# Seven half-size products for eight in the first feed-forward product, with its result kept in DRAM

## The chip, the core and the metric

The kernel runs on one core of one Trainium2 chip. The metric is the device time of one execution in microseconds, as the median of several runs.

## What is computed

One encoder block on 512 tokens of 2048 channels, all in float32: a modulated norm, a wide input projection, two mixers (state space and Fourier), a gated merge, an output projection, and then a SwiGLU feed-forward part. Only the last part matters here:

```python
h2 = modulate(rms_norm(x, norm_ffn[l]), sh_f, sc_f)          # 512 x 2048
a, b = jnp.split(h2 @ w_ffn_in[l], 2, axis=-1)                 # 2048 x (2 * 5632)
x = x + g_f[:, None, :] * ((jax.nn.silu(a) * b) @ w_ffn_out[l])  # 5632 x 2048
return rms_norm(x, norm_final)
```

## The kernel before

Every large product is made from split operands: a float32 matrix is held as `hi` (its value rounded to the format that TensorE reads at full rate, `F32R`) and `lo` (what the rounding left). `split` (line 121) makes them: ScalarE copies to `hi` (L122), VectorE subtracts to `lo` (L123). `mm3` (line 194) issues three matmuls for one product: `hi` by `hi`, `hi` by `lo`, `lo` by `hi` (L196, L197, L198).

The program is a list of steps. Each step has a job (the load of a block of weights of 512 KB, and its preparation, mostly a split) and a function that issues the matmuls. `run_plan` (line 151) writes the steps out: loads go out as early as the slots of a ring of five raw tiles allow, preparations up to three steps ahead (`LOOKAHEAD`). TensorE and GpSimd keep the order written; the orders of ScalarE and VectorE are laid down when the program is built, by priority and expected readiness. SyncE issues the weight loads in order.

The first feed-forward product has 88 output tiles of 128 channels: 44 of `a` and 44 of `b`. `first_fn` (line 1431) makes the first four tiles while the normed input `h2` (16 pairs of `hi` and `lo` tiles, 128 channels by 512 tokens) is still being formed. From line 1455 each tile is made by `ntile` (line 467) in two steps; a step has 8 of the 16 parts of the contraction, that is 24 matmuls with 128x128 weights and 512 moving columns, into one PSUM bank. Then `silu_epi` (line 1398, ScalarE, L1401) or `g_epi` (line 1405, VectorE, L1407) takes the tile out of PSUM, and `g`, the product of the two, stays in SBUF (44 x 512 floats for each partition). Between the tiles 32 steps of `gf_q` (line 1410) form the last modulation vector on VectorE (L283), with 512 KB of weights each, and four times `ada_fin` (line 323) has TensorE add it up.

`fo_open` (line 1462) has GpSimd load what the end needs. Then the second product runs twice over the 44 parts of its contraction, once for each half of the output columns: `fo_job` (line 1485) loads 512 KB of weights and splits them and a tile of `g`; the matmuls (L1509 to L1511) fill all eight PSUM banks (`fo_alloc`, line 1513).

Of the kernel before, what the change touches and what calls it, by code (L numbers as in the profile page):

```python
# [11 lines left out]
F32 = mybir.dt.float32  # L12
F32R = mybir.dt.float32r
# [6 lines left out]
P = 128  # L20
# [31 lines left out]
def encoder_block(ctx: ExitStack, tc: tile.TileContext, x, c, w_ada, b_ada, norm_mix, w_in,  # L52
# [44 lines left out]
    CAP = {"raw": RAW_BUFS, "wh": WH_BUFS, "araw": ARAW_BUFS, "bw": 2, "rv": 2, "acc": 1, "acc2": 2}  # L97

    class Job:
        """A load, and a preparation of what it brought; `raw`, `keep`: the ring slots that each takes.  # L100
        `lead`: steps that the load comes earlier in order; `late`: steps that the result is kept longer.
        The raw slots are free when the job has been prepared (those of `raw_free`), or when it has run
        (`hold`); the others when it has run."""

        def __init__(self, load, prep, raw=(("raw", 1),), keep=(("wh", 1),), raw_free=None, hold=False, free=None):
            self.lead = self.late = 0
            self.load, self.prep, self.raw = load, prep, raw
# [37 lines left out]
    def step(job, fn, barrier=False):  # L145
        """One step of the plan; no weights are prepared ahead of a barrier."""
        if barrier:
            barriers.add(len(steps))
        steps.append((job, fn))

    def run_plan():
# [3 lines left out]
        ld = pp = 0  # L155
# [3 lines left out]
        def fits(slots):  # L159
            return all(used[r] + k <= CAP[r] for r, k in slots)  # L160

# [4 lines left out]
        for i in range(n):  # L166
            moved = True
            while moved:
                moved = False
                while ld < len(order) and fits(steps[order[ld]][0].raw):  # L170
                    j = order[ld]
                    take(steps[j][0].raw, 1)
# [4 lines left out]
                while pp < n and pp <= i + LOOKAHEAD and not (pp in barriers and pp >= i) and (  # L177
                        steps[pp][0] is None or (pp in arrived and fits(steps[pp][0].acq))):
                    job = steps[pp][0]
                    if job is not None:  # L180
                        take(job.acq, 1)
                        prepped[pp] = job.prep(loaded.pop(pp))
                        take(job.at_prep, -1)
# [47 lines left out]
    def bcast_cols(r, dst):  # L231
        """[P, 4] over (token in a tile, tile) -> a row of 512 tokens on every partition."""
# [13 lines left out]
    sgr = drp.tile([KT, P], F32, name="sgr")  # L246

# [1 line left out]
    ada_acc = {}  # L249

    def ada_job(sec, c0, width, q, start=False):
        """Part q of a block of columns: some rows of each partition's 16."""
# [37 lines left out]
        return Job(load, prep, raw=(("araw" if start else "raw", 1),), keep=slot if q == 0 else (),  # L290
                   free=slot if q == parts - 1 else ())

    def ada_pe(width, then):
        """The first columns of the scale, on the tensor engine."""
# [40 lines left out]
    def ada_steps(sec, c0, width=S, start=False, then=None):  # L335
# [5 lines left out]
        return [(ada_job(sec, c0, width, q, start), last if q == parts - 1 else nop) for q in range(parts)]  # L341

# [55 lines left out]
    # The shift of the modulation comes later than its scale: the first output tiles are computed  # L398
    # without it, and what it adds to them is a vector.
# [67 lines left out]
    def ntile(wv, n0, acts, epilogue, inter=None):  # L467
        """Two steps: 128 output channels from column n0 over a contraction of 2048; `inter` is called
        after each of the 16 parts of the contraction."""
# [18 lines left out]
    def spread(tile_steps, extra):  # L488
        """The extra steps behind the two of a tile, evenly."""
# [14 lines left out]
    class Deferred:  # L504
        """Vector operations that are issued a few at a time."""
# [1125 lines left out]
```

## Time and profile before

| | |
|---|---|
| median of 3 runs | 2599.86 us (2590.38 to 2600.63) |
| span of the profiled execution | 2596.6 us |
| TensorE busy in it | 2494.6 us (96%) |
| VectorE, ScalarE, GpSimd busy | 1327.8, 763.0, 415.2 us |
| moved by DMA | 399.32 MB |

The profiled execution has no time of its own beside its span; the span lies within the runs, 3.3 us under their median. Matmuls are pipelined, so that a record of a matmul overlaps the next one's, and "busy" says only that there was no gap. What a matmul costs is read from the distance between the starts of two of them. The trace calls the engines PE (TensorE matmuls), PEld (its weight loads), DVE (VectorE), ACT (ScalarE), POOL (GpSimd) and SP (SyncE).

### The profile page before, as it was taken

Reading aid. Unit: us, or ns where it says so; the run is one execution under the profiler, and the core shown is the slowest. Engines: PE = TensorE matmul, PEld = TensorE weight load, DVE = VectorE, ACT = ScalarE, POOL = GpSimd, SP = SyncE. Lnnn points to the kernel's source line nnn. Section 1 sums busy time; section 2 is a strip of 40 time slices with the busy share of each in tenths; the row PEclk is TensorE's granted clock in tenths of the full one; section 3 lists DMA queues with packets and bytes.
Section 4 is the critical chain, followed back from the end, with each engine's and each line's share of the span. In section 5 each row is a group of like instructions: output and inputs, shape, how many; then the busy total and the mean of one; then the engine's idle time right before and its main releaser. Section 6 shows DMA issues by size and latency. Waiting matters only on the chain.

```text
span 2596.6 us, 29781 instructions
## 1 busy us (share of the span) xinstructions
PE 2494.6 (96%) x11595; PEld 2069.6 (80%) x11595; DVE 1327.8 (51%) x1718; ACT 763.0 (29%) x1097; POOL 415.2 (16%) x523
## 2 busy tenths in 40 slices
PE   6989899899999899999999999999999999999997
PEld 5767687788888787788888888888888888888886
DVE  6988467537667987773333333333322233345335
ACT  4434333243223422252222222222222222223223
POOL 2441989500005410000000000000000030001001
PEclk7989899999999999999999999999999999999999
DMA  8796522558774668863443434444433352333222
GB/s 309 260 313 142 126 78 84 177 154 266 244 219 153 186 216 282 270 204 114 122 122 117 121 113 130 122 119 120 121 97 96 97 195 97 97 98 98 98 97 81
DMA packets 460253, 399.32 MB, mean 154 GB/s; under 512 B 46384, under 2 KB 372544, under 8 KB 460112
## 3 DMA queue, kind: packets, MB, share of 16 engines
q1 hardware_dynamic: 428720, 361.60, 45.1%
q10 hardware_dynamic: 21952, 18.96, 2.7%
q0 software_dynamic: 9440, 16.86, 1.9%
q8 instruction: 91, 1.49, 0.2%
q14 instruction: 50, 0.41, 0.1%
HBM read 372.10 MB, written 29.37 MB: 155 GB/s over the span
## 4 chain that ended last, share of the span: by engine, by line
PE 67%; DVE 11%; DMA 9%; POOL 6%; issue 4%; ACT 2%; SPq 0%; ACTq 0%; DVEq 0%; POOLq 0%
PE ps_acc L196 15%; PE ps_acc L198 15%; PE ps_acc L197 15%; DMA raw<-in_w_in_dram 3%; PE ps_acc L1510 3%; PE ps_acc L1511 3%; PE ps_acc L1509 3%; DVE wlo L123 3%; DMA raw<-in_w_out_dram 3%; DVE ada L283 2%; PE ps_accb L1509 1%; PE ps_m L1509 1%; PE ps_m L1511 1%; PE ps_m L1510 1%; PE ps_accb L1511 1%
## 5 line engine op out<-in xcount | busy, mean ns | idle before, releaser
L123 DVE TENSOR_TENSOR wlo<-raw,whi 128x1024 fp32r<-128x1024 f32 (+2 forms) x424 | 521.6, 1232 | 593.4 <-ACT whi L122 592.9
L122 ACT CAST whi<-raw 128x1024 fp32r<-128x1024 f32 (+2 forms) x424 | 428.4, 1011 | 1043.3 <-PE ps_acc L197 767.4
L198 PE MATMUL ps_acc<-actB,wlo 128*128 128x512 f32 x1776 | 698.0, 393 | 7.6 <-DVE wlo L123 7.6
L196 PE MATMUL ps_acc<-actB,whi 128*128 128x512 f32 x1776 | 703.2, 396 | 1.0 <-ACT actB L122 0.5
L197 PE MATMUL ps_acc<-actB,whi 128*128 128x512 f32 x1776 | 697.4, 393 | 0.9 <-DVE actB L123 0.9
L198 PEld LDWEIGHTS ps_acc<-actB,wlo 128*128 128x128 f32 x1776 | 337.0, 190 | 82.0 <-DVE wlo L123 10.6
L196 PEld LDWEIGHTS ps_acc<-actB,whi 128*128 128x128 f32 x1776 | 337.7, 190 | 72.8 <-issue 2.5
L197 PEld LDWEIGHTS ps_acc<-actB,whi 128*128 128x128 f32 x1776 | 337.1, 190 | 69.6 <-DVE actB L123 1.6
L196 PE MATMUL ps_acc<-actA,whi 128*128 128x512 f32 x592 | 237.9, 402 | 2.1 <-ACT actA L122 2.1
L198 PE MATMUL ps_acc<-actA,wlo 128*128 128x512 f32 x592 | 235.4, 398 | 2.2 <-DVE wlo L123 2.1
L283 DVE SCALAR_TENSOR_TENSOR ada<-raw,c_s,ada 128x512 f32<-128x512 f32 x240 | 181.2, 755 | 108.6 <-DMA raw<-in_w_ada_dram 104.1
L197 PE MATMUL ps_acc<-actA,whi 128*128 128x512 f32 x592 | 235.5, 398 | 0.9 <-DVE actA L123 0.9
L123 DVE TENSOR_TENSOR actA<-g,actA 128x512 fp32r<-128x512 f32 x88 | 61.9, 708 | 260.6 <-ACT actA L122 260.6
L1467 POOL DMA_DIRECT2D sgr<-gr x1 | 0.5, 541 | 1186.4 <-ACT gr L1466 1186.4
L122 ACT CAST actA<-g 128x512 fp32r<-128x512 f32 x88 | 54.5, 623 | 310.8 <-PE ps_m L1510 310.8
L1510 PE MATMUL ps_acc<-wlo,actA 128*128 128x512 f32 x352 | 137.2, 390 | 0.8 <-DVE wlo L123 0.8
L1509 PE MATMUL ps_acc<-whi,actA 128*128 128x512 f32 x352 | 137.1, 389 | 0.0
L1511 PE MATMUL ps_acc<-whi,actA 128*128 128x512 f32 x352 | 137.0, 389 | 0.0
L198 PEld LDWEIGHTS ps_acc<-actA,wlo 128*128 128x128 f32 x592 | 113.9, 192 | 27.8 <-DVE wlo L123 3.4
L196 PEld LDWEIGHTS ps_acc<-actA,whi 128*128 128x128 f32 x592 | 113.4, 192 | 25.6 <-ACT actA L122 2.2
L197 PEld LDWEIGHTS ps_acc<-actA,whi 128*128 128x128 f32 x592 | 113.6, 192 | 24.0 <-DVE actA L123 1.4
L1407 DVE TENSOR_TENSOR g<-silu,ps_acc 128x512 f32<-128x512 f32 x44 | 30.3, 688 | 124.9 <-PE ps_acc L198 124.9
(391 smaller groups left out, 3165.8 us busy)
## 6 DMA issues: line engine op xcount, KB each, us to landing
raw<-in_w_ffn_in_dram SPq DMA_DIRECT2D x168, 512.0 KB
raw<-in_w_ada_dram SPq DMA_DIRECT2D x128, 512.0 KB
raw<-in_w_in_dram SPq DMA_DIRECT2D x108, 512.0 KB
raw<-in_w_ffn_out_dram SPq DMA_DIRECT2D x88, 512.0 KB
araw<-in_w_ada_dram SPq DMA_DIRECT2D x64, 512.0 KB
raw<-in_w_out_dram SPq DMA_DIRECT2D x32, 512.0 KB
raw<-in_w_in_dram SPq DMA_DIRECT2D x16, 384.0 KB
rv<-wrev SPq DMA_DIRECT2D x16, 384.0 KB
```

Source lines behind the costliest of these rows:

```text
L122: A.copy(hi, src)
L123: V.tensor_tensor(out=lo, in0=src, in1=hi.bitcast(F32), op=ALU.subtract)
L196: PE.matmul(o, whi, ahi, start=start, stop=False)
L197: PE.matmul(o, whi, alo, start=False, stop=False)
L198: PE.matmul(o, wlo, ahi, start=False, stop=stop)
L283: V.scalar_tensor_tensor(out=acc, in0=r[:, k, :], scalar=sc, in1=acc, op0=ALU.mult, op1=ALU.add)
L1407: V.tensor_tensor(out=ff["g"][:, j, :], in0=ff.pop(("s", j)), in1=pt, op=ALU.mult)
L1467: nc.gpsimd.dma_start(out=sgr, in_=gr)
L1509: PE.matmul(o, gh[:, ts_], hi[:, cs], start=(k == 0), stop=False)
L1510: PE.matmul(o, gh[:, ts_], lo[:, cs], start=False, stop=False)
L1511: PE.matmul(o, gl[:, ts_], hi[:, cs], start=False, stop=(k == NF - 1))
```

## The change

Of the 88 output tiles of the first feed-forward product, 8 (of `a` and `b`, j under 4) are made as before, and the other 80 in 40 pairs of neighbours. For one pair the 256 output channels, the 512 tokens and the 2048 channels of the contraction are each cut in two, and the eight products of halves are replaced by seven products of sums and differences of halves. `form_sums` makes the four combinations of `h2` once, beside the direct tiles j = 2 and 3. `quad_job` loads 512 KB of weights (a quarter of the contraction for 256 channels), takes three of their four blocks as they are (`hi` by a ScalarE copy; `lo` as a negated ScalarE copy of the rounded value, to which a DMA issued by GpSimd adds the raw value), and makes four combinations of the blocks on VectorE, which are split as before. Each quarter is 42 matmuls of 256 moving columns. After four quarters the pair is put together from PSUM by one ScalarE and five VectorE instructions into two SBUF tiles.

`g` is written to DRAM (`sg`) by DMAs that ScalarE issues, and `fo_job` loads it again, one tile of 256 KB with each block of weights, in both passes. The planner gets slots for this, and a rule that a raw slot stays free for the sums. The diff, without removed comments and less some bookkeeping:

```diff
+           "quad": 3, "ada": 1, "sum": 2, "gr": 2}
...
-                while ld < len(order) and fits(steps[order[ld]][0].raw):
+                while ld < len(order):
                     j = order[ld]
+                    job = steps[j][0]
+                    if not fits((*job.raw, ("raw", 1)) if job.raw and (open_ or job.opens) else job.raw):
+                        break
+                    open_ += job.opens
...
+                        open_ -= job.closes
...
+    sg = drp.tile([NF, P, S], F32, name="sg")
...
     step(None, norm2)
+    DIRECT = 4
+    H = S // 2
+    def ab_tile():
+        return ff["p"].tile([P, S], F32, tag="ab", bufs=4, name="ab")
     def silu_epi(j):
         def fn(pt):
-            s = cpool.tile([P, S], F32, tag="tmp", bufs=3, name="silu")
+            s = ff["s", j] = ab_tile()
             A.activation(out=s, in_=pt, func=AF.Silu)
-            ff["s", j] = s
         return fn
     def g_epi(j):
         def fn(pt):
-            V.tensor_tensor(out=ff["g"][:, j, :], in0=ff.pop(("s", j)), in1=pt, op=ALU.mult)
+            s = ff.pop(("s", j))
+            V.tensor_tensor(out=s, in0=s, in1=pt, op=ALU.mult)
+            A.dma_start(out=sg[j], in_=s)
         return fn
-    gf_q = [st_ for cb in range(4) for st_ in ada_steps(5, cb * S)]
+    def form_sums(p):
+        f = ff["p"].tile([P, 2, 2, H], F32, tag="hT", bufs=2, name="h2f")
+        for i in range(2):
+            hi, lo = h2[2 * p + i]
+            V.tensor_tensor(out=f[:, i].rearrange("p a b -> p (a b)"), in0=hi.bitcast(F32), in1=lo.bitcast(F32),
+                            op=ALU.add)
+        a12, a22, a11, a21 = f[:, 0, 0], f[:, 0, 1], f[:, 1, 0], f[:, 1, 1]
+        t = ff["p"].tile([P, 4, H], F32, tag="lT", bufs=2, name="sumf")
+        V.tensor_tensor(out=t[:, 0], in0=a21, in1=a22, op=ALU.subtract)
+        V.tensor_tensor(out=t[:, 2], in0=a11, in1=a21, op=ALU.subtract)
+        V.tensor_tensor(out=t[:, 1], in0=a11, in1=t[:, 0], op=ALU.subtract)
+        V.tensor_tensor(out=t[:, 3], in0=t[:, 1], in1=a12, op=ALU.subtract)
+        hl = [ff["p"].tile([P, 4, H], F32R, name=f"sum{p}{i}") for i in range(2)]
+        split(hl[0], hl[1], t)
+        ff["S", p] = hl
+    def quad_job(c, n0):
+        st = {}
+        def load():
+            st["r"] = raw_tile([P, 2, 4, P])
+            nc.sync.dma_start(out=st["r"].rearrange("p a (b n) c -> p (a b) (n c)", b=2),
+                              in_=w_fi_v[:, 4 * c:4 * c + 4, n0:n0 + 2 * P])
+            return st["r"]
+        def prep(r):
+            hi, lo = hl_tiles([P, 2, 3, P])
+            A.copy(hi, r[:, :, 0:3])
+            A.activation(out=lo, in_=r[:, :, 0:3], func=AF.Copy, scale=-1.0)
+            G.dma_start(out=lo, in_=r[:, :, 0:3], accum_op=ALU.add)
+            st["w"] = (hi, lo)
+        job = Job(load, prep, raw=(("raw", 1), ("quad", 1)), raw_free=())
+        job.late, job.opens = 1, True
+        def prep_sums(_):
+            r = st["r"]
+            t = raw_tile([P, 2, 4, P])
+            V.tensor_tensor(out=t[:, :, 0:2], in0=r[:, :, 1:3], in1=r[:, :, 3:4].to_broadcast([P, 2, 2, P]), op=ALU.add)
+            V.tensor_tensor(out=t[:, :, 2], in0=t[:, :, 1], in1=r[:, :, 1], op=ALU.add)
+            V.tensor_tensor(out=t[:, :, 3], in0=t[:, :, 2], in1=r[:, :, 0], op=ALU.add)
+            hi = ff["p"].tile([P, 2, 4, P], F32R, tag="hT", bufs=2, name="hT")
+            lo = ff["p"].tile([P, 2, 4, P], F32R, tag="lT", bufs=2, name="lT")
+            split(hi, lo, t)
+            return (*st["w"], hi, lo)
+        sums = Job(lambda: None, prep_sums, raw=(), keep=(("sum", 1), ("raw", 1)), raw_free=(("raw", 2), ("quad", 1)),
+                   free=(("sum", 1),))
+        sums.closes = True
+        return job, sums
+    def quad_tiles(n0, epilogue):
+        st = {}
+        def fn_of(c):
+            def fn(w):
+                hr, lr, ht, lt = w
+                if c == 0:
+                    st["37"], st["24"], st["16"], st["5"] = (
+                        f((P, 2, H)) for f in (ps_acc, ps_acc, ps_b, ps_m))
+                plan = [("16", 0, True, (hr, lr), 2, None, (1, 0)), ("24", 0, True, (hr, lr), 0, None, (0, 0)),
+                        ("37", 0, True, (hr, lr), 1, 3, None), ("5", 0, True, (ht, lt), 1, 0, None),
+                        ("37", 1, False, (ht, lt), 0, 2, None), ("16", 1, False, (ht, lt), 2, 1, None),
+                        ("24", 1, False, (ht, lt), 3, None, (0, 1))]
+                for bank, half, opens, (wh, wl), q, s_, raw in plan:
+                    o = st[bank][:, half]
+                    for i in range(2):
+                        p = 2 * c + i
+                        if raw is None:
+                            ah, al = (x[:, s_] for x in ff["S", p])
+                        else:
+                            ah, al = (x[:, raw[1] * H:(raw[1] + 1) * H] for x in h2[2 * p + raw[0]])
+                        first, last = c == 0 and i == 0, c == 3 and i == 1
+                        PE.matmul(o, wh[:, i, q], ah, start=first and opens, stop=False, skip_group_check=True)
+                        PE.matmul(o, wh[:, i, q], al, start=False, stop=False, skip_group_check=True)
+                        PE.matmul(o, wl[:, i, q], ah, start=False, stop=last, skip_group_check=True)
+                if c < 3:
+                    return
+                ez = cpool.tile([P, 2, H], F32, tag="tmp", bufs=3, name="ez")
+                uw = cpool.tile([P, 2, H], F32, tag="tmp", bufs=3, name="uw")
+                A.copy(ez[:, 0], st["16"][:, 0])
+                V.tensor_tensor(out=uw[:, 0], in0=st["16"][:, 1], in1=ez[:, 0], op=ALU.subtract)
+                V.tensor_tensor(out=uw[:, 1], in0=st["5"][:, 0], in1=uw[:, 0], op=ALU.add)
+                V.tensor_tensor(out=ez[:, 1], in0=st["37"][:, 1], in1=uw[:, 0], op=ALU.subtract)
+                b2 = ab_tile()
+                V.tensor_tensor(out=b2.rearrange("p (a b) -> p a b", a=2), in0=uw[:, 1:2].to_broadcast([P, 2, H]),
+                                in1=st["37"], op=ALU.subtract)
+                a2 = ab_tile()
+                V.tensor_tensor(out=a2.rearrange("p (a b) -> p a b", a=2), in0=st["24"], in1=ez, op=ALU.add)
+                epilogue(a2, b2)
+            return fn
+        out_ = []
+        for c in range(4):
+            job, sums = quad_job(c, n0)
+            out_ += [(job, nop), (sums, fn_of(c))]
+        return out_
+    def silu2(j):
+        def fn(*tiles):
+            for i, t in enumerate(tiles):
+                A.activation(out=t, in_=t, func=AF.Silu)
+                ff["s", j + i] = t
+        return fn
+    def g2(j):
+        def fn(*tiles):
+            for i, t in enumerate(tiles):
+                g_epi(j + i)(t)
+        return fn
+    gf_q = [st_ for cb in range(4) for st_ in ada_steps(5, cb * S, extra=(("ada", 1),))]
     pairs = [(ntile(w_fi_v, j * P, lambda: h2, silu_epi(j)), ntile(w_fi_v, DFF + j * P, lambda: h2, g_epi(j)))
-             for j in range(NF)]
+             for j in range(DIRECT)]
     first = []
     def first_job(kk):
...
                     mm3(first[n], (hi[:, k % 2, n % 2, cs], lo[:, k % 2, n % 2, cs]), h2[k], k == 0, k == KT - 1)
             if kk == KT // 2 - 1:
                 x1x.close()
-                ff["g"] = ffx.enter_context(tc.tile_pool(name="ffp", bufs=1)).tile([P, NF, S], F32, name="g")
+                ff["p"] = ffx.enter_context(tc.tile_pool(name="ffp", bufs=1))
                 for j in range(2):
                     silu_epi(j)(first[2 * j])
                     g_epi(j)(first[2 * j + 1])
     for kk in range(KT // 2):
         step(first_job(kk), first_fn(kk))
-    for j in range(2, NF):
-        steps.extend(spread(pairs[j][0], some(gf_q, 1) if j >= 4 else []) + pairs[j][1])
+    for j in range(2, DIRECT):
+        for i, (job, fn) in enumerate(pairs[j][0] + pairs[j][1]):
+            p = 4 * (j - 2) + i
+            step(job, lambda w, fn=fn, p=p: (fn(w), form_sums(p)))
+    for j in range(DIRECT, NF, 2):
+        for n0, epi in ((j * P, silu2(j)), (DFF + j * P, g2(j))):
+            tl = quad_tiles(n0, epi)
+            steps.extend(tl[:4] + some(gf_q, 1) + tl[4:])
     assert not gf_q
     fo = {"x2": {}, "gf": [], "nf": []}
     def fo_open(_):
         def load():
             r = raw_tile([P, 1024])
             nc.sync.dma_start(out=r, in_=src)
-            return r
-        def prep(r):
+            gr = ab_tile()
+            nc.sync.dma_start(out=gr, in_=sg[k])
+            return r, gr
+        def prep(rg):
+            r, gr = rg
             hi, lo = hl_tiles([P, 1024])
             split(hi, lo, r)
             gh, gl = act_tile(0), act_tile(0)
-            split(gh, gl, ff["g"][:, k, :])
+            split(gh, gl, gr)
             return hi, lo, gh, gl
-        job = Job(load, prep)
+        job = Job(load, prep, raw=(("raw", 1), ("gr", 1)))
         job.late = NF - 1 - k if k >= NF - LAST[half] else 0
         return job
```

## Rows read from the trace of the kernel before

**Rows 1.** The page's first lines: the span, and TensorE's busy time.
```profile
span 2596.6 us, 29781 instructions
...
PE 2494.6 (96%) x11595; PEld 2069.6 (80%) x11595; DVE 1327.8 (51%) x1718; ACT 763.0 (29%) x1097; POOL 415.2 (16%) x523
```
**Rows 2.** Stretches: start, first product (two), second product; columns as in the header.
```profile
core 0: us, PE busy (x) PEld busy (x) DVE busy (x) ACT busy (x) POOL busy (x), PEclk, DMA share, GB/s
0.00:200.00 200.00, 163.95 (x707) 135.08 (x708) 167.58 (x318) 84.30 (x134) 75.66 (x57) 0.87 0.86 293
1180.00:2094.00 914.00, 914.00 (x4050) 757.50 (x4049) 280.59 (x282) 199.86 (x216) 0.00 (x0) 1.00 0.39 115
1250.00:1450.00 200.00, 200.00 (x889) 165.75 (x888) 64.05 (x65) 42.27 (x45) 0.00 (x0) 1.00 0.41 120
2140.00:2330.00 190.00, 190.00 (x840) 157.38 (x839) 67.15 (x70) 54.65 (x70) 0.00 (x0) 1.00 0.30 97
```
**Rows 3.** Waits from 1200 to 2100 us; engine, line, waited for: total us, times, longest.
```profile
ACT whi L122 <- PE ps_acc L197: 705.0, 165, 5.3
DVE wlo L123 <- ACT whi L122: 388.0, 132, 5.1
...
SPq L135 <- DVE wlo L123: 477.4, 127, 5.9
```
**Rows 4.** Timeline of TensorE, first product: two starts, 24 matmuls apart.
```profile
1580.08 0.39 PE L197 MATMUL ps_acc<-actB,whi 128*128 128x512 f32 x1
...
1585.52 0.39 PE L197 MATMUL ps_acc<-actB,whi 128*128 128x512 f32 x1
```
**Rows 5.** Timeline of TensorE, branch product: two starts, 17 matmuls of 258 columns apart.
```profile
910.74 0.28 PE L196 MATMUL ps_accb<-ab,whi 128*128 128x258 f32 x1
...
912.78 0.28 PE L198 MATMUL ps_accb<-ab,wlo 128*128 128x258 f32 x1
```
**Rows 6.** Groups from 1180 to 2094 us, shapes apart: count, busy us, mean ns, idle before.
```profile
L123 DVE TENSOR_TENSOR wlo<-raw,whi 128x1024 fp32r<-128x1024 f32 x168 | 205.7, 1224 | 398.9 <-ACT whi L122 398.7
L196 PEld LDWEIGHTS ps_acc<-actB,whi 128*128 128x128 f32 x1003 | 188.3, 188 | 38.8
L122 ACT CAST whi<-raw 128x1024 fp32r<-128x1024 f32 x167 | 175.3, 1050 | 712.0 <-PE ps_acc L197 712.0
L283 DVE SCALAR_TENSOR_TENSOR ada<-raw,c_s,ada 128x512 f32<-128x512 f32 x60 | 45.1, 752 | 97.1 <-DMA raw<-in_w_ada_dram 96.0
L1407 DVE TENSOR_TENSOR g<-silu,ps_acc 128x512 f32<-128x512 f32 x43 | 29.6, 687 | 121.6 <-PE ps_acc L198 121.6
L1401 ACT ACTIVATE silu<-ps_acc 128x512 f32<-128x512 f32 x44 | 26.0, 591 | 2.0 <-PE ps_acc L198 2.0
```
**Rows 7.** Groups of the whole span, shapes apart: other sizes on VectorE and ScalarE.
```profile
L123 DVE TENSOR_TENSOR actA<-g,actA 128x512 fp32r<-128x512 f32 x88 | 61.9, 708 | 260.6 <-ACT actA L122 260.6
L123 DVE TENSOR_TENSOR wlo<-wp,whi 128x768 fp32r<-128x768 f32 x16 | 24.7, 1541 | 2.5 <-ACT whi L122 2.4
L123 DVE TENSOR_TENSOR blo<-rv,bhi 128x768 fp32r<-128x768 f32 x16 | 15.0, 940 | 0.0
L123 DVE TENSOR_TENSOR ab<-ps_accb,ab 128x258 fp32r<-128x258 f32 x12 | 5.0, 423 | 13.4 <-ACT ab L122 13.4
...
L122 ACT CAST bhi<-rv 128x768 fp32r<-128x768 f32 x16 | 13.3, 832 | 6.2 <-POOL rv L1247 6.2
L122 ACT CAST v<-ps_m 128x258 fp32r<-128x258 f32 x24 | 9.0, 373 | 33.0 <-PE ps_m L198 33.0
```
**Rows 8.** Groups of GpSimd: DMAs that it issues, by program line.
```profile
L1476 POOL DMA_DIRECT2D actB<-sx x16 | 8.7, 547 | 6.6 <-DMA actB<-in_norm_final_dram 3.4 <-issue 1.7 <-DMA actB<-sx 1.0
L998 POOL DMA_DIRECT2D wrev<-in_w_branch_fnet_dram x6 | 6.8, 1138 | 0.0
```
**Rows 9.** DMA issues: what, queue, count, KB each, median us to landing.
```profile
wrev<-in_w_branch_fnet_dram POOLq DMA_DIRECT2D x6, 1016.0 KB, 19.8
...
sxT<-xT POOLq DMA_DIRECT2D x4, 1024.0 KB, 6.1
```
**Rows 10.** Timeline where the products meet: VectorE beside DMAs that GpSimd issues.
```profile
2101.37 0.69 DVE L1407 TENSOR_TENSOR g<-silu,ps_acc 128x512 f32<-128x512 f32 x1 [3.36 <-PE ps_acc L198]
...
2108.34 1.23 DVE L123 TENSOR_TENSOR wlo<-raw,whi 128x1024 fp32r<-128x1024 f32 x1 [0.26 <-ACT whi L122]
...
2108.45 1.62 POOL L1471 DMA_DIRECT2D actB<-in_norm_final_dram  x3
```

More of the change, by code (lines that the diff above doesn't have):

```diff
@@ L95, in encoder_block @@
     barriers = set()
-    CAP = {"raw": RAW_BUFS, "wh": WH_BUFS, "araw": ARAW_BUFS, "bw": 2, "rv": 2, "acc": 1, "acc2": 2}
+    CAP = {"raw": RAW_BUFS, "wh": WH_BUFS, "araw": ARAW_BUFS, "bw": 2, "rv": 2, "acc": 1, "acc2": 2,
+           "quad": 3, "ada": 1, "sum": 2, "gr": 2}
     class Job:
@@ L106, in __init__ @@
             self.lead = self.late = 0
+            self.opens = self.closes = False
             self.load, self.prep, self.raw = load, prep, raw
@@ L154, in run_plan @@
         used = dict.fromkeys(CAP, 0)
-        ld = pp = 0
+        ld = pp = open_ = 0
         order = sorted((i for i in range(n) if steps[i][0] is not None), key=lambda i: (i - steps[i][0].lead, i))
@@ L159, in fits @@
         def fits(slots):
-            return all(used[r] + k <= CAP[r] for r, k in slots)
+            need = {}
+            for r, k in slots:
+                need[r] = need.get(r, 0) + k
+            return all(used[r] + k <= CAP[r] for r, k in need.items())
         def take(slots, sign):
@@ L246, in encoder_block, with ada_job @@
     sgr = drp.tile([KT, P], F32, name="sgr")
+    sg = drp.tile([NF, P, S], F32, name="sg")
     ada_acc = {}
-    def ada_job(sec, c0, width, q, start=False):
+    def ada_job(sec, c0, width, q, start=False, extra=()):
         rows_ = 1024 // width
@@ L289, in ada_job @@
         slot = (("acc2" if start else "acc", 1),)
-        return Job(load, prep, raw=(("araw" if start else "raw", 1),), keep=slot if q == 0 else (),
+        return Job(load, prep, raw=(("araw" if start else "raw", 1), *extra), keep=slot if q == 0 else (),
                    free=slot if q == parts - 1 else ())
@@ L333, in nop, with ada_steps @@
         pass
-    def ada_steps(sec, c0, width=S, start=False, then=None):
+    def ada_steps(sec, c0, width=S, start=False, then=None, extra=()):
         def last(_):
@@ L340, in ada_steps @@
         parts = KT * width // 1024
-        return [(ada_job(sec, c0, width, q, start), last if q == parts - 1 else nop) for q in range(parts)]
+        return [(ada_job(sec, c0, width, q, start, extra), last if q == parts - 1 else nop) for q in range(parts)]
     s5x = ExitStack()
```

## The prediction, as it was put on record

> **What bounds the kernel now.** I read the page's engine line first, then the stretches, then who waits for whom, and last the timeline of TensorE. TensorE is busy for 96% of the span [rows 1], and in the first feed-forward product, from 1180 to 2094 us, for all of it, at a granted clock of 1.00, which is the level of 2.4 GHz; VectorE has 281 of these 914 us, ScalarE 200, GpSimd nothing, and the DMA engines are taken 0.39 of the time [rows 2]. The waits say the same: ScalarE waits 705 us for TensorE to give a weight buffer back, VectorE for ScalarE, and SyncE for VectorE to free a raw tile [rows 3]. Everything is early and TensorE sets the end. So a microsecond of TensorE taken out here is a microsecond of the kernel, as long as the others stay early.
>
> **What TensorE saves.** Two starts that lie 24 matmuls apart differ by 5.44 us: a matmul of 512 columns costs 0.2267 us [rows 4]. Two tiles of 128 channels take 2 x 16 x 3 = 96 of them, 21.76 us; 40 such pairs 870.5 us. After the change a pair takes 4 quarters x 7 products x 2 x 3 = 168 matmuls of 256 columns. The nearest row has 258 columns, the same 128x128 weights and the same three matmuls for a product: 17 of them in 2.04 us, 0.1200 us each [rows 5]. The 254 columns between the two rows cost 0.1067 us, so two columns less is 0.1192 us, and 12 ns of each matmul do not shrink with it. A pair then takes 20.03 us, 40 pairs 801 us, and the saving is 69.5 us, or 1.73 us a pair. Seven for eight alone would give 870.5 / 8 = 109 us; 40 us of it go into the fixed 12 ns. I take the measured spacing.
>
> There are 72 more weight loads in a pair. Their record lasts 188 ns [rows 6], but a matmul of 258 columns with a new load each time still starts every 120 ns [rows 5], so loads are hidden at this width. The Trainium skill (TensorE: Matmul & The Clock Gate, "The mechanism" in Part 3) says that a weight load overlaps running matmuls only where its row group differs; by this, loads of all 128 rows would not be hidden, and the change would lose. The spacing in this trace speaks against it; as a rival it stands below.
>
> **What VectorE gets.** In each quarter (5.01 us of TensorE): sums of weights of 512, 256 and 256 elements, 0.71 + 2 x 0.42 us, and the subtraction for the split of 1024, 1.22 us [rows 6, 7]; 2.77 us. For each pair: three PSUM instructions of 256 at 0.42 and two of 512 at 0.69, 2.64 us; half of two products for g at 0.71, 0.71 us; and in 32 of 40 pairs two steps of the modulation at 0.75, 1.50 us [rows 6, 7]. Together 4 x 2.77 + 4.85 = 15.9 of 20.03 us, 80%. That is twice as full as before and still not the bound. A row of 768 elements that took 0.94 us took 1.54 us where GpSimd computed beside it [rows 7]; times 1.64 VectorE would need 26 us a pair and be the bound. But GpSimd only issues DMAs here, and beside those a subtraction of 1024 took 1.23 us [rows 10], the same as 1.22. I take 80%.
>
> Does it come in time? The buffers of the split sums come in two, so those of quarter c+1 can be written when quarter c-1 has ended, and are first read by the fourth of the seven products of c+1, 5.01 + 18 x 0.119 = 7.2 us later. The worst quarter is the first of a pair: the five PSUM instructions (ScalarE 0.37, then 2.64 us), the two products for g (1.4), and then the subtraction (1.22) end after some 5.9 us with the hops between engines. That is 1.3 us early. The next quarter has 12 us for two subtractions and the sums. So I put the cost of VectorE at nothing; if its work were a quarter longer this cover would be gone, and the 1 to 2 us a pair that are late would eat the 1.73 us.
>
> **ScalarE and its queue.** Two copies of 768 (0.83 each) and one of 1024 (1.05) in a quarter, one of 256 (0.37) and one silu (0.59) a pair [rows 6, 7]: 11.8 of 20.03 us. The stores of g wait in its queue for VectorE's product; the copies for the next quarters stand behind them, with over 5 us to spare. Two stores in 40 us: nothing.
>
> **The accumulating DMA** is the one price that the trace does not have. Per quarter GpSimd issues one DMA that adds 384 KB of raw values into `lo`. Issuing costs 0.55 to 1.14 us [rows 8] of an idle engine. The move itself: from below, 1024 KB from SBUF land in 6.1 us, 2.3 us for 384 KB; from above, 1016 KB from DRAM to DRAM land in 19.8 us, 7.5 us for 384 KB [rows 9]. A gain is excluded, since the bytes were not moved before. An addition has to read both sides, so I take twice the lower value, 4.6 us, the SBUF row being the nearer one. It has to fit into 5.01 us, and it does; about two quarters of lead hide its latency.
>
> Seen as a share of the DMA engines: 120 GB/s took 0.41 with 512-byte rows and 97 GB/s took 0.30 with 4 KB rows [rows 2], so all of them move 293 to 323 GB/s; I take 308. Weights need 105 GB/s, the modulation 26, the stores of g 13: 144, or 0.47. The accumulation's 78.5 GB/s are 0.255 as a copy and 0.51 as two: 0.98 in all. This is at the edge. The start of the kernel ran at 0.86 and 293 GB/s [rows 2]. I put 5 us for queueing (bounds 0 and 25).
>
> The Trainium skill (Collectives: The Full Stack, "The bandwidth ceiling") says that an adding transfer is slower than a copy since it needs two source reads, and reports the ratio as 1.93. No run here shows it yet; by it the share would be 0.96.
>
> **The rest.** Eight `form_sums` put 4.3 us of VectorE beside each 5.44 us step that has 1.22 already: 0.1 us too much in each step, needed only later; 2 us (0 to 4). At the end of the last pair two of four first-tag banks are held until its five VectorE instructions are done, 3 us, against 1.4 us of matmuls that have banks; 2 us. Before, that tile's product of 0.69 us [rows 10] held one bank. The second product loads 256 KB more for each 512 KB on SyncE's queue: 145 GB/s or 0.47 of the engines in place of 0.30, with two loads ahead, over 10 us; nothing. `fo_open`'s DMAs on GpSimd queue behind the last accumulations, done by then.
>
> Sum on the profiled execution: 2596.6 - 69.5 + 5 + 2 + 2 = 2536. The runs' median is 3.3 us over its span, so 2539 for a measured time.
>
> **The rivals.**
> A. The accumulation costs more than two copies, the DMA engines become the bound, and TensorE waits for `lo`. It decides where 0.47 + 0.255 k, times 801 us, exceeds 870.5 us: k = 2.42 copies, or 5.44 us for one DMA. At k = 3 the share is 1.235, the stage 989 us, and the kernel 2600 + 119 + 4 = 2723; at the upper row's 7.5 us it is 1200 us, some 2930. For it: the estimate at k = 2 has no margin. Against: the low row already holds fixed time and other traffic. Chance 0.22; this is the slower one.
> B. The cover on VectorE is thin: chains between ScalarE and VectorE or a DMA share a little above 1 eat 0.6 to 1.7 us a pair. Time 2563 to 2607, around 2585. For it: 80% and a static order, and the DMA share of 0.98. Against: 1.3 us of slack in the worst quarter. Chance 0.20, half within 0.5%.
> C. The change does not do what it says: 256 columns do not come at 0.119 us, because weight loads show. 72 x 0.188 = 13.5 us a pair, 541 us in all, some 3070. The row of 258 columns speaks against it. Chance 0.02.
> My forecast, 2520 to 2560: 0.56.
>
> **How the numbers follow.** 0.5% is 13 us, about what a measurement of this kernel tells from no change. Faster by more: 0.56 + 0.10 = 0.66; within: 0.10; slower: 0.22 + 0.02 = 0.24. The predicted time is the forecast's, 2539. The low end 2518 is the saving with the 12 ns a little smaller and no new cost. The high end leaves out the dear half of A: 2.6 copies give a stage of 908 us, 2641; I take 2650.
>
> **What would show it.** Right: 256-column matmuls 0.119 us apart, a pair every 20 us, the granted clock at 1.00, VectorE at 80% and the DMA share near 0.95 in the stage, the second product as long as before. For A: gaps before the matmul that reads `lo`, released by the DMA on GpSimd's queue, a landing time over 10 us, a share of 1. For B: gaps before the fourth product, released by the subtraction on VectorE. For C: no gaps, but a wider spacing. The forecast is wrong if a quarter takes over 5.4 us.

## The result and the profile after

| | before | changed |
|---|---|---|
| median | 2595.47 us (2590.38 to 2600.63, 4 runs) | 2563.39 us (2557.31 to 2566.06, 4 runs) |
| ratio, with its 95% interval | | 0.9863 (0.9837 to 0.9889) |
| span of the profiled execution | 2596.6 us | 2561.7 us |
| first feed-forward product in it | 962.5 us | 928.2 us |

The kernel is faster by 32 us, where 61 were forecast. The time lies 3 us past the forecast's own range (2520 to 2560), at the cheap end of rival B (2563 to 2607). Of the 34.9 us between the two spans 34.3 lie in the first product; the work behind it takes 496.1 us in place of 495.2.

First the page of the changed kernel: span, engines, and the one group that is new in kind, with its DMA issue.

```profile
span 2561.7 us, 37880 instructions
...
PE 2437.8 (95%) x14475; PEld 2157.9 (84%) x14475; DVE 1674.1 (65%) x2454; ACT 1030.5 (40%) x1465; POOL 605.9 (24%) x683
...
L1463 POOL DMA_DIRECT2D wlo<-raw x160 | 192.4, 1203 | 948.6 <-ACT wlo L1462 566.6
...
wlo<-raw POOLq DMA_DIRECT2D x160, 384.0 KB, 5.7
```

Next the timeline of TensorE in the changed kernel, two starts that lie 35 matmuls of 256 columns apart.

```profile
1457.73 0.28 PE L1509 MATMUL ps_acc<-sum,hT 128*128 128x256 f32 x1
...
1461.93 0.28 PE L1511 MATMUL ps_acc<-sum,wlo 128*128 128x256 f32 x1
```

4.20 us for 35 of them: 0.1200 us each, as the 258 columns of [rows 5], and a pair of 168 takes 20.16 us. Read pair by pair from the starts, 20 of the 40 take 20.15 or 20.16 us. The others take 20.5 to 25.9.

The stretches say which pairs those are. In the view below (start, end and length; then the busy time of each engine with its count of records, the granted clock, the DMA share and GB/s) the row from 1900 us holds the last eight pairs. They have the same quarters and the same accumulating DMAs as all others, and no modulation step. The row below it is from the second product.

```profile
core 0: us, PE busy (x) PEld busy (x) DVE busy (x) ACT busy (x) POOL busy (x), PEclk, DMA share, GB/s
1230.00:1390.00 160.00, 154.99 (x1252) 154.17 (x1251) 107.23 (x173) 82.41 (x103) 35.83 (x30) 0.97 0.87 205
1390.00:1550.00 160.00, 156.34 (x1282) 155.28 (x1281) 116.26 (x188) 85.05 (x108) 36.06 (x30) 0.99 0.88 211
1550.00:1710.00 160.00, 156.17 (x1293) 155.03 (x1291) 110.33 (x179) 80.95 (x103) 36.06 (x30) 1.00 0.89 213
...
1900.00:2060.00 160.00, 160.00 (x1336) 160.00 (x1335) 110.47 (x175) 91.44 (x114) 36.07 (x30) 1.00 0.87 199
...
2100.00:2300.00 200.00, 200.00 (x884) 165.68 (x883) 73.05 (x79) 57.69 (x76) 1.48 (x1) 1.00 0.46 150
```

TensorE stands still for 3.7 to 5.0 us in each 160 us of modulated pairs, and not at all in the last eight. VectorE is as full in both, and so are the DMA engines (0.87 to 0.89). The second product has the 0.46 that was forecast as 0.47, and no gap.

The 839.9 us of the 40 pairs therefore divide into 806.4 at 0.1200 us, 24.7 in 28 gaps of more than 0.15 us, and 8.8 in matmuls that start further apart than 0.12 us without a gap, 6.4 of them at the lower clock that is shown below. Of the gaps 3.2 us belong to the ends of modulation blocks, which the kernel before has too. The other 21.5 stand in or just ahead of the fourth product of a pair's last quarter.

Who waits for whom, changed kernel, 1180 to 2060 us (engine, line, waited for: total us, times, longest):

```profile
POOL wlo L1463 <- ACT wlo L1462: 566.6, 133, 10.2
ACT hT L124 <- DVE raw L1474: 174.0, 56, 8.8
DVE ada L295 <- DMA raw<-in_w_ada_dram: 125.0, 28, 7.2
DVE lT L125 <- ACT hT L124: 78.9, 47, 5.3
...
PE ps_m L1511 <- DVE lT L125: 9.7, 14, 0.8
...
PE ps_m L1509 <- ACT hT L124: 7.6, 6, 2.3
```

and SyncE's own queue, 1230 to 2060 us:

```profile
SPq L1455 <- DMA wlo<-raw: 391.1, 91, 9.0
SPq L1455 <- DMA raw<-in_w_ada_dram: 178.7, 28, 8.5
SPq L1455 <- DVE raw L1474: 112.9, 44, 3.2
```

Before, SyncE waited for VectorE's subtraction to free a raw tile [rows 3]. Now what it waits for most is the accumulating DMA, which is the last to read the tile. VectorE waits 4.5 us at 28 of the 32 modulation steps for their 512 KB. Before, it waited 96.0 us for the same loads [rows 6], and there it cost nothing, since VectorE was busy for 281 of 914 us [rows 2].

One such gap, from the timeline of the changed kernel (start, length, engine, line, operation; in brackets the idle time before it and what ended it):

```profile
1444.11 0.61 SPq L273 DMA_DIRECT2D raw<-in_w_ada_dram  x1
...
1446.13 0.69 DVE L1472 TENSOR_TENSOR raw<-raw 128x512 f32<-128x512 f32 x1
1452.60 0.75 DVE L295 SCALAR_TENSOR_TENSOR ada<-raw,c_s,ada 128x512 f32<-128x512 f32 x1 [5.78 <-DMA raw<-in_w_ada_dram]
1453.27 0.42 DVE L1473 TENSOR_TENSOR raw<-raw 128x256 f32<-128x256 f32 x1
1453.61 0.75 DVE L295 SCALAR_TENSOR_TENSOR ada<-raw,c_s,ada 128x512 f32<-128x512 f32 x1
1454.27 0.42 DVE L1474 TENSOR_TENSOR raw<-raw 128x256 f32<-128x256 f32 x1
...
1454.80 1.05 ACT L124 CAST hT<-raw 128x1024 fp32r<-128x1024 f32 x1 [7.32 <-DVE raw L1474]
...
1455.88 1.22 DVE L125 TENSOR_TENSOR lT<-raw,hT 128x1024 fp32r<-128x1024 f32 x1
...
1456.12 0.28 PE L1510 MATMUL ps_m<-sum,hT 128*128 128x256 f32 x1
1457.16 0.39 PE L1511 MATMUL ps_m<-sum,lT 128*128 128x256 f32 x1 [0.76 <-DVE lT L125]
```

The sums of this quarter are three VectorE instructions, L1472 to L1474. The modulation step stands between the first and the second of them in VectorE's order, and its weights come 5.78 us late. So the third sum ends at 1454.7, the rounding on ScalarE at 1455.9, the subtraction at 1457.1, and TensorE, which needs its result, stops.

After the larger gaps the clock adds to the loss. Two stretches of the changed kernel, columns as above:

```profile
1348.00:1351.00 3.00, 0.50 (x2) 0.30 (x2) 2.90 (x6) 2.02 (x3) 0.00 (x0) 0.93 0.50 172
1351.00:1359.00 8.00, 7.67 (x42) 7.67 (x43) 7.76 (x16) 4.49 (x7) 2.40 (x2) 0.60 0.86 171
```

TensorE idled for 2.5 of 3 us, and then ran at a mean granted clock of 0.60, mostly at 0.5, which is the level of 1.2 GHz, before it was back at 1.00. In those 8 us it did 42 matmuls, which take 5.0 us at 0.12. This happened four times, for 3.4 to 6.8 us each.

### The profile page after: what moved, and what is told of

Read it like the earlier page. It is cut to its first block, busy times and chain, and to the rows that moved or that the text cites. A ratio compares the mean times of both kernels' runs of the same rounds, so it can differ in the third digit from the quotient of the medians.

```text
span 2561.7 us, 37880 instructions
## 1 busy us (share of the span) xinstructions
PE 2437.8 (95%) x14475; PEld 2157.9 (84%) x14475; DVE 1674.1 (65%) x2454; ACT 1030.5 (40%) x1465; POOL 605.9 (24%) x683
## 4 chain that ended last, share of the span: by engine, by line
PE 50%; DVE 18%; DMA 14%; issue 7%; POOL 6%; ACT 4%; SPq 0%; ACTq 0%; DVEq 0%; POOLq 0%
DMA raw<-in_w_ada_dram 6%; PE ps_acc L207 4%; PE ps_acc L208 4%; PE ps_acc L209 4%; DMA raw<-in_w_out_dram 3%; PE ps_acc L1656 3%; PE ps_acc L1655 3%; PE ps_acc L1657 3%; DVE ada L295 3%; DVE wlo L125 3%; PE ps_acc L1509 3%; PE ps_acc L1510 3%; PE ps_acc L1511 3%; DMA raw<-in_w_in_dram 2%; DVE lT L125 2%
## 5 line engine op out<-in xcount | busy, mean ns | idle before, releaser
L125 DVE TENSOR_TENSOR wlo<-raw,whi 128x1024 fp32r<-128x1024 f32 (+2 forms) x264 | 324.8, 1232 | 191.1 <-ACT whi L124 190.3
L1463 POOL DMA_DIRECT2D wlo<-raw x160 | 192.4, 1203 | 948.6 <-ACT wlo L1462 566.6
L124 ACT CAST whi<-raw 128x1024 fp32r<-128x1024 f32 (+2 forms) x264 | 260.5, 988 | 326.9 <-DMA raw<-in_w_out_dram 104.6
L209 PE MATMUL ps_acc<-actB,wlo 128*128 128x512 f32 x816 | 324.9, 398 | 8.1 <-DVE wlo L125 8.1
L207 PE MATMUL ps_acc<-actB,whi 128*128 128x512 f32 x816 | 329.9, 404 | 1.9 <-ACT whi L124 1.5
L208 PE MATMUL ps_acc<-actB,whi 128*128 128x512 f32 x816 | 324.1, 397 | 0.3 <-DVE actB L125 0.3
L124 ACT CAST hT<-raw 128x1024 fp32r<-128x1024 f32 x160 | 167.6, 1047 | 258.4 <-DVE raw L1474 174.0
L125 DVE TENSOR_TENSOR lT<-raw,hT 128x1024 fp32r<-128x1024 f32 x160 | 195.5, 1222 | 79.2 <-ACT hT L124 78.9
L209 PEld LDWEIGHTS ps_acc<-actB,wlo 128*128 128x128 f32 x816 | 156.9, 192 | 45.3 <-DVE wlo L125 11.3
L207 PEld LDWEIGHTS ps_acc<-actB,whi 128*128 128x128 f32 x816 | 157.8, 193 | 37.0 <-ACT whi L124 2.7
L208 PEld LDWEIGHTS ps_acc<-actB,whi 128*128 128x128 f32 x816 | 157.1, 193 | 31.4 <-DVE actB L125 0.6
L1472 DVE TENSOR_TENSOR raw<-raw 128x512 f32<-128x512 f32 x160 | 110.6, 691 | 18.9 <-DMA wlo<-raw 14.0
L207 PE MATMUL ps_acc<-actA,whi 128*128 128x512 f32 x272 | 112.9, 415 | 2.1 <-ACT actA L124 2.1
```

Source lines behind the costliest of these rows:

```text
L124: A.copy(hi, src)
L125: V.tensor_tensor(out=lo, in0=src, in1=hi.bitcast(F32), op=ALU.subtract)
L207: PE.matmul(o, whi, ahi, start=start, stop=False)
L208: PE.matmul(o, whi, alo, start=False, stop=False)
L209: PE.matmul(o, wlo, ahi, start=False, stop=stop)
L1463: G.dma_start(out=lo, in_=r[:, :, 0:3], accum_op=ALU.add)
```

## The experiments

The first expectation below names three theories, W, D and V. Two more came later and are not the rivals of the prediction. Theory S: the accumulating DMA holds the raw tile until it lands, so the ring of five tiles comes free late, SyncE's loads go out late, and the modulation step, fixed in VectorE's order, makes the sums behind it late. Theory B: the DMA engines or VectorE are too full, and any more work or bytes at this place makes gaps. All ratios are to the kernel before, with 95% intervals, and "the stage" is the 40 pairs, from the first matmul of 256 columns to the last.

### The modulation steps left out

```diff
+    V.memset(mod[5], 0.0)
...
-            steps.extend(tl[:4] + some(gf_q, 1) + tl[4:])
-    assert not gf_q
+            steps.extend(tl)
```

> Leaves out the 32 steps that form the last modulation vector in this stage (their loads, 64 VectorE instructions, 4 small groups on TensorE); the vector is zero. Theory W (VectorE stands in its fixed order before a modulation instruction whose 512 KB have not landed, 125 us in all, and the sums of the pair's last quarter come late): the stage of seven products falls from 840 us to about 807, no gaps before the fourth product of the last quarter, the clock stays at 1.00; kernel 2526 to 2534. Rival D (the DMA engines, at 0.88, are too slow for the accumulation): the share falls only by 0.08, most gaps stay; 2548 to 2560. Rival V (VectorE has too much work): as W, since 1.5 us of work a pair goes too.

2528.3 us, 0.9721 (0.9702 to 0.9741). The stage takes 806.4 us, every pair 20.16. The stretch from 1230 us on, and below it SyncE's wait in it:

```profile
1230.00:1890.00 660.00, 660.00 (x5502) 660.00 (x5502) 457.46 (x725) 373.51 (x460) 157.42 (x131) 1.00 0.87 196
```

```profile
SPq L1456 <- DMA wlo<-raw: 560.1, 115, 9.1
```

The accumulation alone, at a DMA share of 0.87 and with SyncE waiting for it even longer, costs TensorE nothing. It takes a modulation step beside it to make a gap. That rules out D as it was put, a DMA too slow for its work; W and V had forecast this time alike.

### The accumulating DMA left out

```diff
-            G.dma_start(out=lo, in_=r[:, :, 0:3], accum_op=ALU.add)
```

> Leaves out the accumulating DMA, so that lo is only the negated rounded value; all else stays. Rival D: all gaps go, 2524 to 2532. Theory W: the DMA share falls to about 0.45, so modulation loads land in 4 us rather than 8 and raw tiles come free earlier; part of the gaps goes, 2530 to 2550, and VectorE still waits some 50 us for those loads. Rival V: little change, 2555 to 2565.

2534.69 us, 0.9744 (0.9727 to 0.9761). The stage takes 809.9 us and has no gap but the 3.2 us at the ends of modulation blocks. Waits of this kernel, 1230 to 2060 us, then its stretch from 1230 us:

```profile
DVE ada L295 <- DMA raw<-in_w_ada_dram: 1.6, 3, 0.9
```

```profile
1230.00:1890.00 660.00, 660.00 (x5505) 660.00 (x5504) 487.63 (x782) 370.51 (x455) 0.00 (x0) 1.00 0.44 142
```

VectorE's wait for the modulation falls from 125.0 to 1.6 us. The time rules out V and misses D by 3 us; it lies in W's range, though W had left some 50 us of that wait. This run takes away hold and traffic together, and so does not tell S from B.

### The same DMA from another source

The DMA adds a tile that stays in place, of the same size, in place of the raw tile. The traffic remains and the raw tile is no longer held.

```diff
-            G.dma_start(out=lo, in_=r[:, :, 0:3], accum_op=ALU.add)
+            G.dma_start(out=lo..., in_=ff["S", 0][0]...[:, 0:768], accum_op=ALU.add)
```

> The accumulating DMA stays, with the same 384 KB and the same wait for lo, but it adds a fixed tile of sums instead of the raw weights, so that it no longer holds a raw tile (lo is wrong by that). Theory S (the DMA is the last reader of a raw tile, so the ring of five comes free late and the loads behind it, the modulation's above all, go out late): the gaps go, 2530 to 2542, and SyncE's waits for that DMA vanish. Theory B (its traffic, at a share of 0.88, makes every load land late): as the changed kernel, 2557 to 2568, VectorE waits over 80 us for modulation loads.

2532.44 us, 0.9739 (0.9718 to 0.9761); the stage 809.9 us, no gaps but those 3.2 us. Stretch, then VectorE's and SyncE's waits in it:

```profile
1230.00:1890.00 660.00, 660.00 (x5505) 660.00 (x5504) 486.83 (x781) 367.87 (x455) 114.28 (x131) 1.00 0.89 220
```

```profile
DVE ada L295 <- DMA raw<-in_w_ada_dram: 65.6, 28, 6.1
```

```profile
SPq L1455 <- DVE raw L1474: 295.8, 116, 6.8
```

The DMA engines are as full as in the changed kernel (0.89), the DMA lands after 6.0 us in place of 5.7, and yet the loss is gone. SyncE no longer waits for the DMA but for VectorE. VectorE still waits for the modulation, half as long, and that much does no harm. (Each of these DMAs moves the same bytes in 143 packets in place of 270; together they take 45% of the engines' time, as before.) So this traffic without the hold costs nothing here, as S has it and B has not. The traffic has a part all the same. Read from the starts, as medians over 31 pairs: the modulation's load goes out 8.9 us before TensorE begins the last quarter in the changed kernel, 10.1 us here and 11.3 us without the DMA; VectorE begins with it 6.3, 5.8 and 3.6 us later. The traffic uses up half of the time in hand, and the hold takes the rest. That a hold would do it without traffic is not shown.

### The subtraction back on VectorE

```diff
-            A.copy(hi, r[:, :, 0:3])
-            A.activation(out=lo, in_=r[:, :, 0:3], func=AF.Copy, scale=-1.0)
-            G.dma_start(out=lo, in_=r[:, :, 0:3], accum_op=ALU.add)
+            split(hi, lo, r[:, :, 0:3])
```

> lo of the three plain blocks is made by a VectorE subtraction of 768 elements, as elsewhere in the kernel, in place of a ScalarE copy and the accumulating DMA. VectorE gets 0.94 us more in each quarter: 15.9 + 3.8 = 19.7 of 20.0 us a pair. Theory W and rival V: VectorE is the bound, a pair takes 21 to 23 us, kernel 2590 to 2670. Rival D: the DMA share falls to 0.45 and the gaps go, 2525 to 2540.

2537.15 us, 0.9753 (0.973 to 0.9776); the stage 809.9 us, no gaps but those 3.2 us. Its stretch:

```profile
1230.00:1890.00 660.00, 660.00 (x5505) 660.00 (x5504) 592.87 (x911) 273.67 (x325) 0.00 (x0) 1.00 0.44 142
```

My expectation for W and V missed; the time is the one of D, which the modulation run had ruled out. VectorE is busy for 90% and TensorE never waits. So how full VectorE is does not decide alone. One thing more differs: since VectorE's orders are laid down by priority, the modulation step stands elsewhere. Counted from the end of the pair before, three sum instructions come ahead of it in 18 of 31 pairs; in the changed kernel it is one or none in 27. What that gives is not separated from the missing DMA. In a further measurement this kernel and the changed one ran on one chip.

> The changed kernel again, beside the next one on the same chip: 2557 to 2567.

> The version with the VectorE subtraction again, as the version that beats both: 2530 to 2540, 0.9 to 1.2% under the changed kernel.

The changed kernel: 2559.64 us, 0.9831 (0.9806 to 0.9856). With the subtraction on VectorE: 2536.54 us, 0.9752 (0.9733 to 0.9772). The intervals lie apart. So the negated copy and the accumulating DMA were not needed: without them the kernel takes 0.9% less than the changed one beside it, and 2.5% less than the one before.

### Traffic without a hold, on a fuller VectorE

The same edit, and each quarter two plain DMAs of 384 KB from `hi` to DRAM.

```diff
+    scr = drp.tile([8, P, 768], F32, name="scr")
...
+            split(hi, lo, r[:, :, 0:3])
+            for i_ in range(2):
+                G.dma_start(out=scr[2 * (scn[0] % 4) + i_], in_=hi...)
...
```

> The version with the VectorE subtraction (2537), plus two plain DMAs a quarter that copy the 384 KB of hi to DRAM and that nothing waits for: about the engine time of one accumulation, but no raw tile held. Theory B: the loss comes back, 2555 to 2570, with VectorE waiting over 60 us for modulation loads. Theory S: 2533 to 2545 at a DMA share of 0.8 to 0.9.

2549.31 us, 0.9809 (0.9791 to 0.9828); the stage 824.2 us with 15.2 us of gaps. Stretch and wait:

```profile
1230.00:1890.00 660.00, 650.70 (x5386) 646.82 (x5386) 576.83 (x893) 259.48 (x319) 137.11 (x256) 1.00 0.85 292
```

```profile
DVE ada L297 <- DMA raw<-in_w_ada_dram: 64.6, 28, 4.6
```

Between the ranges of the two theories. Nothing holds a raw tile here, but at 292 GB/s VectorE waits for the modulation for as long as in the kernel with the other source (65 us in all), and on a VectorE that is nearly full (576.83 of 660 us) this costs 12 us against the same kernel without the copies, whose order on VectorE is the same. So traffic alone can do it too. That VectorE had no room to catch up is the likely reason, since the other source had the same wait and no loss; but the modulation step also stands elsewhere in its order there.

### A hold without an accumulation

The subtraction on VectorE, and per quarter two chained DMAs of 128 KB from the raw tile into a spare tile, after a copy of one element on ScalarE into that tile.

```diff
...
+            sp = ff["p"].tile([P, 2, P], F32, tag="spare", bufs=1, name="spare")
+            A.copy(sp[:, 0, 0:1], hi[:, 0, 0, 0:1].bitcast(F32))
+            for i_ in range(2):
+                G.dma_start(out=sp, in_=r[:, i_, 0:2])
```

> The version with the VectorE subtraction, plus two small DMAs a quarter, one behind the other, that copy 128 KB each out of the raw tile and start after hi: a third less traffic than the accumulation's reads and writes, but the raw tile is held until they have landed, as by the accumulation. Theory S (held raw tiles make the loss): SyncE waits over 150 us for these DMAs, VectorE over 60 us for modulation loads, gaps before the fourth product come back, 2542 to 2562, at a DMA share under 0.75. Theory B (traffic): 2533 to 2541, as without them.

2755.99 us, 1.059 (1.0564 to 1.0617); the stage 1036 us, past both ranges. ScalarE's and VectorE's waits, then the stretch, 1230 to 1890 us:

```profile
ACT spare L1463 <- DMA spare<-raw: 286.9, 100, 6.2
...
DVE raw L1474 <- DMA spare<-raw: 108.2, 60, 4.3
```

```profile
1230.00:1890.00 660.00, 577.70 (x4304) 564.81 (x4303) 460.28 (x710) 225.50 (x356) 111.70 (x203) 0.91 0.47 151
```

A large loss at a DMA share of 0.47, so bytes are not what makes it. VectorE's first sum waits 108 us for a raw tile that these DMAs still read, so a hold can stop VectorE as well as SyncE. But ScalarE itself waits 287 us for the spare tile, ahead of its copies for the weights, and most of the gaps (136.7 of 159.8 us) moved to the fourth product of the second quarter. The run does not measure the hold alone and does not decide between the theories.

### The modulation's loads earlier

```diff
+    for job, _ in gf_q:
+        job.lead = 4
```

> The same work as the changed kernel; only the loads of the 32 modulation steps stand four steps (two quarters) earlier in SyncE's queue. Theory W: VectorE's wait for these loads falls from 125 us to under 30, the gaps before the fourth product go, and the kernel takes 2530 to 2540. Rival V (too much work on VectorE): no change, 2557 to 2566, since the work is the same. Rival D: no change, or slower by up to 10 us, since a raw tile is held longer.

2574.17 us, 0.9891 (0.9869 to 0.9913): not faster. VectorE's wait from 1230 to 1890 us is hardly shorter, and the gaps stand in the third quarter of the pair, no longer in the fourth:

```profile
DVE ada L295 <- DMA raw<-in_w_ada_dram: 112.7, 28, 5.9
```

```profile
1230.00:1890.00 660.00, 633.97 (x5160) 627.31 (x5158) 451.11 (x732) 340.88 (x426) 146.59 (x122) 0.99 0.87 206
```

Theory W missed; rival D's forecast, up to 10 us slower, comes nearest. The step's VectorE instructions moved forward with its load: in 27 of 31 pairs one subtraction stands between the end of the pair before and the modulation step, where the changed kernel has two. The load goes out 14.3 us before the last quarter in place of 8.9, and VectorE begins with it 8.4 us before in place of 2.3 (medians). So the load is no earlier for the instruction that waits for it; no run holds the load early and the instructions late.

### Only the way through DRAM, and fewer columns

All 88 tiles direct as before, and only `g` through DRAM:

```diff
-    DIRECT = 4
+    DIRECT = NF
...
```

> All 88 tiles direct as before; only g goes through DRAM. By the prediction the DRAM route costs nothing: 2594 to 2606, within 0.3% of the kernel before. Rival: two loads ahead instead of five, and 50% more bytes in the second product, leave TensorE waiting there: over 2610.

2596.2 us, 0.999 (0.9977 to 1.0002, 10 runs). The way through DRAM costs nothing, as the prediction had it.

Last, the kernel with the subtraction on VectorE, with 192 moving columns for 256 in the second and third quarter of each pair:

```diff
...
+                    nw = 192 if c in (1, 2) else H
...
```

> The version with the VectorE subtraction; in quarters 1 and 2 of each pair the matmuls have 192 moving columns in place of 256 (a quarter of the tokens left out there). If the spacing is columns plus a fixed part, as between 258 and 512 columns, 192 columns start every 0.092 to 0.094 us and VectorE becomes the bound (gaps). If a weight load takes 0.120 us whatever the columns, the spacing of 0.120 stays and nothing changes, 2533 to 2540.

2499.37 us in one run. Timeline of TensorE in the second quarter:

```profile
1400.42 0.25 PE L1508 MATMUL ps_accb<-actB,whi 128*128 128x192 f32 x1
...
1403.98 0.27 PE L1510 MATMUL ps_accb<-sum,lT 128*128 128x192 f32 x1
```

and its busy times in that stretch, columns as above:

```profile
1400.40:1405.00 4.60, 4.60 (x44) 4.60 (x42) 3.22 (x5) 1.88 (x2) 0.00 (x0) 1.00 0.35 118
```

The distance is 0.111 us (32 matmuls in 3.56 us), where the line through 258 and 512 columns would give 0.092. Neither expectation was met: the distance is neither 0.092 nor 0.120, and no gap came. A quarter fewer columns saves 7%.

## Why the prediction was right, and where it failed

**What bounds the kernel.** Right. Wherever the inputs were in time (four kernels), TensorE ran without a gap, and what it saved came out whole.

**What TensorE saves.** The right row, a wrong correction. The step took 0.1192 us for 256 columns, from 0.1200 for 258 and a slope; it is 0.1200. That is 0.13 us a pair, 5.4 us in all. From 512 to 256 columns the distance falls by 0.1067 us, 0.417 ns for each column, which leaves 13 ns that do not shrink, close to the 12 of the prediction. At 192 columns (0.111 us) the same slope leaves 31 ns. So the fixed part held for this change and does not hold below it.

The rival about weight loads (C) fell, and with it the sentence of the Trainium skill that was weighed there (TensorE: Matmul & The Clock Gate, "The mechanism" in Part 3): 128x128 loads and 256-column matmuls run side by side at 0.1200 us, with the load unit busy for 660.00 of 660 us.

**VectorE.** The cost of nothing for its amount of work was right: 74% in the kernel with the accumulation left out (487.63 of 660 us), 80% forecast. The sentence that a quarter more work would end the cover found no support: with 22% more (592.87 us for 487.63), at 90%, there was no gap. The 1.54 us that were taken for a subtraction beside a computing GpSimd is a mean: in the trace of before, seven of these 16 ran beside GpSimd's instructions and took 1.8 to 2.6 us, the other nine 0.94 to 0.95; in this stage GpSimd does not compute, so nothing hangs on it. What the step left out of its sum is what the static order, named under rival B, does with a late input. A wait of one instruction for a DMA delays all behind it, and the 96.0 us of waits for the modulation were in the rows of before already [rows 6], where idle time covered them. The slack of 1.3 us was reckoned for the first quarter of a pair; the gaps came in the last, where the modulation step stands.

**The accumulating DMA.** Its price was nearly right, its effect was missed. In the changed kernel from 1300 to 2000 us (queue: packets, MB, share of 16 engines; then issues):

```profile
q0 software_dynamic: 36241, 52.38, 45.8%
q1 hardware_dynamic: 77515, 83.84, 37.6%
...
wlo<-raw POOLq DMA_DIRECT2D x134, 384.0 KB, 5.7
```

134 of them took 0.458 x 700 us, 2.39 us each of all 16 engines, or 164 GB/s. The loads moved 83.84 MB in 0.376 x 700 us, 318 GB/s. So one addition costs k = 1.94 copies, against the 2 that were taken and the 2.42 from which rival A decides, and close to the 1.93 of the Trainium skill (Collectives: The Full Stack, "The bandwidth ceiling"). The agreement hangs on what is called a copy. Against the 308 GB/s of the prediction k is 1.87; against the plain DMAs from `hi` to DRAM in the run with two of them (1300 to 1880 us, below), 87.91 MB in 0.406 x 580 us or 373 GB/s, it is 2.27. All lie under 2.42. The share is 0.88, not 0.98.

```profile
q0 software_dynamic: 17891, 87.91, 40.6%
```

Landing took 5.7 us, inside the bounds of 2.3 and 7.5.

The step that failed is the next one: "about two quarters of lead hide its latency". This is true for who reads `lo`. It is not true for the raw tile, which stays taken until the DMA lands, while SyncE's loads wait for it in order. Holding a tile is a cost beside moving bytes, and the sum had no term for it. The term for queueing, 5 us with bounds 0 and 25, was the only place for it, and it was too small. With the 2 and 2 for `form_sums` and the last pair the sum had 9 us; what was paid in the stage alone is 839.9 - 806.4 - 3.2 = 30.3 us, and without the hold 0.3 us (809.9 - 806.4 - 3.2). The two small terms came to 1.2 us (the direct tiles took 88.3 us for four times 21.76) and 0.9 (the work behind).

**The rivals.** B happened in its sign: gaps before the fourth product, released by VectorE's subtraction or ScalarE's copy for it, at 30.3 / 40 = 0.76 us a pair, of 0.6 to 1.7 (0.95 for each of the 32 modulated ones). Of its two causes the share above 1 did not come. A chain between VectorE and ScalarE did, but a late load set it off, which B does not name. A's rate did not happen. Without the hold the kernel lands at 2532 to 2537 us in three ways (without the DMA, with its other source, with the subtraction on VectorE), beside the 2539 that was forecast; part of that is luck, two errors that cancel, 5.4 us too little for the spacing and 7 too much for queueing and the two small terms.

**Chances.** Faster by more than 0.5% had 0.66, and the time lies inside the range of 2518 to 2650, which is wide enough to hold B; the forecast's own range, with 0.56, it misses by 3 us. The sign that was to tell a wrong forecast, a quarter over 5.4 us, shows in the last quarters that have a gap, not in the mean of 839.9 / 160 = 5.25 us.

**Open.** No run has the hold without the traffic, so how much of the 30 us it costs alone is not known. What sets the spacing at 192 columns was not found, and that row is from one run.

## What to carry to other kernels

When a copy or a subtraction is given to a DMA, ask what it still reads and until when: its landing time is added to the life of the source tile, and the next loads queue behind that. A wait for a transfer that costs nothing on an engine with time to spare can cost time once that engine feeds the bound in a fixed order: 65.6 us of such waits still cost nothing here, 125.0 us cost 30, and on a fuller VectorE 64.6 us cost 12. Look for such waits in the profile of before, and ask where they stand in the order as well as how full the engine is. Take the spacing of a matmul from the row with the nearest width, and don't extend a line beyond its rows.

## What had not been expected of the hardware

A VectorE that was 90% busy kept TensorE fed without a gap over 660 us, while one that was 67 to 73% busy, with late inputs, did not. Matmuls of 258 and 256 columns with a new 128x128 load each start 0.120 us apart, of 192 columns 0.111 us, of 512 columns 0.227 us. The adding DMA cost 2.39 us of all 16 engines for 384 KB, and landed after 5.7 us. 2.5 us of idle TensorE were followed by 8 us at a mean granted clock of 0.60, mostly at the level of 1.2 GHz, so that part of the price of a gap is paid after it.
